# One more unit of the output projection ahead of the norms, in the first pair of the second feed-forward block

## The chip, the cores and the metric

The kernel runs on one core of one Trainium2 chip. The metric is the device time of one execution in microseconds. Five engines work side by side, each with an in-order queue: TensorE (PE, the matmuls, with their weight loads shown as PEld), VectorE (DVE), ScalarE (ACT), GpSimd (POOL) and SyncE (SP, which here only issues DMAs).

## What is computed

One inference step of one layer over 1024 prompt frames and 32 sample frames, 1056 rows of 1024 channels: a gated feed-forward block, a mixer (differential attention and a gated recurrence) and a second gated feed-forward block, each with a norm before and after it. The part around the change, cut from the reference:

```python
    out = jnp.concatenate([att_out, lru_out], axis=-1) @ w_out
    ...
    x = x + rmsnorm(m, gmb)                       # m is the mixer's out
    x = x + 0.5 * rmsnorm(swiglu(rmsnorm(x, g2a), f2g, f2u, f2d), g2b)
```

with `swiglu(x) = (silu(x @ w_gate) * (x @ w_up)) @ w_down`, an inner width of 2816, and everything in float32.

## The kernel before

Activations lie with channels on the 128 partitions and rows along the free dimension; the 1056 rows are split into two sides of 528 (`SB`) and four parts of 264 (`HB`). A float32 product is made of three matmuls on rounded parts (`mm3`, line 569: high times high, high times low, low times high), each 128x128 by 128x264.

`ffn` (line 852) is one feed-forward block. The inner width is walked in 11 pairs by `gate_up(p)`. Pair 0 of each block is the place where the block's input is made, and it is done in units, one for each of the four parts of the rows. A unit has three steps:

- **begin** (line 1557, second block): the part of the output projection that is still missing. For each of four column pairs c, 30 matmuls into a PSUM tile `po` (two halves, five of the eight inputs k = 7, 0, 1, 2, 3, three matmuls each), then VectorE adds the tile to `y` (line 1563) and `square_sum` squares it on ScalarE and sums it on VectorE into `acc`. A unit is 120 matmuls.
- **end** (line 1566): `boundary` (line 680) with the norm after the mixer. `rstd` (line 629) sums `acc` over partitions on TensorE, VectorE makes the mean (`ms`), GpSimd raises it to the power -1/2 (line 647), TensorE spreads the result over a PSUM tile `st`. Then for each c: load the residual tile `r` by DMA (line 685), scale `y` on VectorE, add `r`, store `y`, square and sum again. A second `rstd` gives the norm ahead of the block, and `scaled` applies it. After that `natural_operands` (line 713) splits the part into rounded high and low tiles `X`: casts on ScalarE, subtractions on VectorE.
- **products** (line 773): 48 matmuls for the gate and 48 for the up projection into PSUM tiles `pq`, with the weights `W`.

The loop at lines 873 to 885 places these: in turn n it writes the begin of unit n, then the end and the products of unit n - lead. With lead = 2 the order written is b0 b1 b2 e0 n0 b3 e1 n1 e2 n2 e3 n3 (b for begin, e for end, n for products). `sums` (line 891) then makes the seven combined operands that the later pairs use for a seven-product scheme (`right_operands`, line 718; `products`, line 805).

The order written is not the order run. A planner (lines 52 to 373) records every operation, finds what it depends on, and schedules all of them with a list scheduler whose priorities come from a backward pass; four rounds of six passes, the shortest modelled plan is kept, and each engine's queue is pinned to it. The order written enters in two ways: as the first priorities, and through the rings of buffers. `Ring` and `take` (lines 108 and 417) give a new tile only a slot whose last use stands earlier in the order written, and of these the one whose tile ends first by the plan of the round before. The tile then waits for that last use. Three rings matter here: `three`, three PSUM slots that `po` and `pq` share; `S`, 45 slots of SBUF that hold `cat` (the mixer's outputs, two slots for each k), `Wo` (the output projection's weights, two for each k), `y`, `X`, `W`, `H` and `r`; and `accp`, four slots for `acc`. While begin steps are still to come, ten slots of `cat` and ten of `Wo` are held.

```python
            lead = 2
            for n in range(len(units) + lead):
                if n < len(units):
                    s, (e, begin, _) = units[n]
                    begin(Z[s])
                if n >= lead:
                    s, (e, _, end) = units[n - lead]
                    ...
```

Of the kernel before, what the change touches and what calls it, by code (L numbers as in the profile page):

```python
# [498 lines left out]
def trunk(ctx: ExitStack, tc: tile.TileContext, plan, xt, w1g, w1u, w1d, w2g, w2u, w2d, win, wv, wout, kpast, vpast,  # L499
# [203 lines left out]
    def halves(t):  # L703

        v = t.rearrange("p a (e r) -> p a e r", e=2)
        return v[:, :, 0], v[:, :, 1]
# [6 lines left out]
    def natural_operands(Z, e, X):  # L713

        for h in range(2):
            X[h, e] = [operand(halves(Z[2 * h + c])[e], "X") for c in range(2)]
# [24 lines left out]
    def left_operands(src, natural=False):  # L741

        raw = []
        for s in src:
            raw.append(S.tile([128, 2, 512], F32, "raw"))
            sp.dma_start(raw[-1].rearrange("p a b -> p (a b)"), s)
        (a11, a12), (a21, a22) = ([r[:, 0], r[:, 1]] for r in raw)
        W = {}

        def make(i, a):  # L750
            t = S.tile([128, 2, 512], FR, "W")
            split((t[:, 0], t[:, 1]), a)
            W[i] = t[:, 0], t[:, 1]

        if natural:
            for k, a in (((0, 0), a11), ((1, 0), a21), ((0, 1), a12), ((1, 1), a22)):
                make(k, a)
            return W
        make(1, a11)
        make(4, a22)  # L760
        s3 = up.tile([128, 512], F32, "s3")
        adder.tensor_sub(s3, a11, a21)
        adder.tensor_add(a22, a21, a22)
        make(5, a22)
        make(2, a12)
        adder.tensor_sub(a11, a22, a11)
        make(6, a11)
        make(7, s3)
        adder.tensor_sub(a12, a12, a11)
        make(3, a12)  # L770
        return W

    def natural_products(ps, W, X, e, out, up_part):

        t = ps.tile([128, 2, 512], F32, "pq")
        for h in range(2):
            for r in range(2):
                for kk in range(4):
                    a, b = X[h, e][kk // 2], kk % 2
                    mm3(t[:, r, :HB], W[r, h], cslice(kk), (a[0][:, b], a[1][:, b]), slice(0, HB),  # L780
                        h == kk == 0, h == 1 and kk == 3)
        for r in range(2):
            if up_part:
                dve.tensor_mul(out[r], out[r], t[:, r, :HB])
            else:
                act.activation(out[r], t[:, r, :HB], AF.Silu)
# [65 lines left out]
    def ffn(tails, stat, sides, wg, wu, wd, cuts, finish, plain, last=False):  # L852
# [4 lines left out]
        def gate_up(p):  # L857
            H = [S.tile([128, 2, SB], F32, "H") for _ in range(2)]
            quarters = halves(H[0]) + halves(H[1])
            if p:  # L860
                for k, w in enumerate((wg, wu)):
                    W = left_operands([w[2 * p], w[2 * p + 1]], p < plain)
                    (natural_quarters if p < plain else products)(stat.four, W, X, quarters, k)
                    if k and p == plain - 1:
                        sums()
                return H, quarters
            W = [left_operands([w[0], w[1]], True) for w in (wg, wu)]
            place = stat.open(2)
            units = [(s, part) for s, tiles, parts in sides for part in parts]
            for s, tiles, _ in sides:  # L870
                Z[s] = tiles()

            lead = 2
            for n in range(len(units) + lead):
                if n < len(units):
                    s, (e, begin, _) = units[n]
# [3 lines that stand above are left out]
                    plan.hurry = HURRY[0]  # L880
                    end(Z[s])
                    natural_operands(Z[s], e, X[s])
                    plan.hurry = 0.0
                    for k in range(2):
                        natural_products(tails, W[k], X[s], e, [quarters[2 * r + e][:, s] for r in range(2)], k)
            place.close()
            if plain == 1:
                sums()
            return H, quarters

        def sums():
            for s, _, _ in sides:
                X[s] = right_operands(Z[s], X[s])
# [262 lines left out]
    def q_item(h):  # L1156
        def evac(p, tb):
            t = tp.tile([128, NT], F32, "tq")
            dve.scalar_tensor_tensor(t, p, -0.125 / SLOPES[h], rb[:, tsl(tb)], op0=ALU.mult, op1=ALU.mult)
            sp.dma_start(q_d[h][:, tsl(tb)], t)  # L1160
        return (h, evac)

    def k_item(h):
        def evac(p, tb):
            t = tp.tile([128, NT], F32, "tk")
            dve.tensor_mul(t, p, rb[:, tsl(tb)])
            sp.dma_start(k_d[h][:, tsl(tb)], t)
            sp.dma_start(k_o[h][:, tsl(tb)], t)
        return (4 + h, evac)
# [97 lines left out]
    def gate_item(c, h):  # L1267
        def evac(p, tb):
            g = tp.tile([128, NT], F32, "gl")
            dve.tensor_mul(g, p, rb[:, tsl(tb)])  # L1270
            act.activation(g, g, AF.Gelu_apprx_tanh)
            a = tb * NT
            n = min(NT, SEQ - a)
            adder.tensor_mul(g[:, :n], g[:, :n], h[:, a:a + n])
            if n < NT:
                adder.tensor_mul(g[:, n:], g[:, n:], h[:, S0:S0 + DEC])
            sp.dma_start(cat_d[4 + c][:, a:a + NT], g)

        return (16 + c, evac)
# [188 lines left out]
    def attend(h, head, stored, before, filler=(), per=0):  # L1468
        filler = iter(filler)
        if not stored:  # L1470
            cat[h] = pair(T, "cat%d" % h)
        for unit in ("s", 3, 2, 1, 0):
            plan.hurry = HURRY[2]
            if unit == "s":
                finish = attention_sample(h, head, cat[h])
            else:
                finish = attention_pair(h, unit, head, cat[h])
            if before is not None:
                before()
            plan.hurry = 0.0  # L1480
            before = finish
            for _ in range(per):
                next(filler, None)
        for _ in filler:
            pass
        return finish
# [11 lines left out]
    def out_group(ks, first):  # L1498
        for c in range(KD // 2):
            for s in range(2):  # L1500
                if first:
                    Y[c, s] = S.tile([128, 2, SB], F32, "y")
                for i in range(2):
                    for e in range(0, SB, HB):
                        p = one.tile([128, HB], F32, "po")
                        at = s * SB + e
                        for n, k in enumerate(ks):
                            mm3(p, Wo[k], cslice(2 * c + i), cat[k], slice(at, at + HB), n == 0, n == len(ks) - 1)
                        y = Y[c, s][:, i, e:e + HB]
                        if first:  # L1510
                            act.copy(y, p)
                        else:
                            dve.tensor_add(y, y, p)
                        yield

    def project_steps(items):
        for a in range(0, len(items), 2):
            yield from project(one, items[a:a + 2])

    def gates(*cs):  # L1520
        return project_steps([gate_item(c, H[c]) for c in cs])

    head = load_head(0)
    last = attend(0, head, True, None, project_steps([q_item(1), k_item(1), q_item(2), k_item(2)]), 3)
    head = load_head(1)
    last = attend(1, head, True, last, project_steps([q_item(3), k_item(3)] + [gate_item(0, H[0])]), 2)
    head = load_head(2)
    last = attend(2, head, False, last, gates(1, 2, 3), 2)
# [4 lines left out]
    last = attend(3, head, False, last, out_group((4, 5, 6), True), 7)  # L1533
# [133 lines left out]
```

## Time and profile before

| | |
|---|---|
| median of 3 runs | 1937.21 us (1936.35 to 1940.25) |
| the profiled execution | 1938.35 us |
| its span, first to last instruction | 1936.5 us |
| TensorE busy | 1901.5 us, 98% |
| VectorE busy | 1404.7 us, 73% |
| ScalarE busy | 685.3 us, 35% |
| GpSimd busy | 62.1 us, 3% |
| mean granted TensorE clock | 0.991 |

The profiled execution's own time is 1.85 us more than its span and 1.14 us above the median of the runs. The trace names every instruction by the tile it writes and the tiles it reads (`po<-cat7l,w` is a matmul of the output projection on the low part of input 7). All of them have line 145, the planner's call, so groups are told apart by tile. "Idle before" is what an engine waited just ahead of an instruction, with the one that released it. The granted clock (PEclk) is a share of full speed: 1.00 stands for 2.4 GHz and 0.50 for 1.2 GHz.

### The profile page before, as it was taken

How to read it: one execution, taken by the hardware profiler on the slowest of the kernel's cores; microseconds unless marked ns; L12 is line 12 of the kernel's file. 1: busy time of each engine (PE TensorE's matmuls, PEld its weight loads, DVE VectorE, ACT ScalarE, POOL GpSimd, SP SyncE). 2: the span in 40 equal slices, each digit the busy share in tenths (PEclk: the TensorE clock that was granted, in tenths of full speed). 3: DMA queues.
4: the chain of work that ended last, by engine and by line, in shares of the span. 5: the costliest groups of instructions: out<-in, count | busy, mean ns of one | idle time of the engine just before them, and what ended most of it. 6: DMA issues, size and time to landing. Idle time of an engine off the chain costs nothing.

```text
span 1936.5 us, 35396 instructions
## 1 busy us (share of the span) xinstructions
PE 1901.5 (98%) x14540; PEld 1861.9 (96%) x14540; DVE 1404.7 (73%) x2548; ACT 685.3 (35%) x1362; POOL 62.1 (3%) x79
## 2 busy tenths in 40 slices
PE   9999999999999999999999999999999999999997
PEld 8999999999999999988889899999999999999997
DVE  7866677665888587875767868886766666688847
ACT  7422222223233044453557655542222222333302
POOL 0000000000000001110000001100000000000000
PEclk9999999999999999999999999999999999999998
DMA  3332333324634243243452342323332223553442
GB/s 135 94 94 84 105 101 106 104 84 150 209 115 150 89 127 126 89 138 116 138 148 65 118 154 69 101 94 112 100 111 95 84 90 110 190 185 125 128 136 90
DMA packets 127810, 225.62 MB, mean 117 GB/s; under 512 B 11424, under 2 KB 84896, under 8 KB 127648
## 3 DMA queue, kind: packets, MB, share of 16 engines
q1 hardware_dynamic: 127504, 223.31, 36.3%
q8 instruction: 114, 1.87, 0.4%
q14 instruction: 48, 0.39, 0.1%
q10 hardware_dynamic: 144, 0.05, 0.0%
HBM read 157.48 MB, written 65.83 MB: 115 GB/s over the span
## 4 chain that ended last, share of the span: by engine, by line
PE 89%; DVE 5%; DMA 3%; ACT 1%; issue 1%; POOL 0%; SPq 0%; POOLq 0%; DVEq 0%; ACTq 0%
PE pq L145 43%; PE pd L145 19%; PE pp L145 8%; PE pe L145 5%; PE po L145 4%; PE pv L145 3%; PE st L145 3%; DVE y L145 1%; DVE W L145 1%; PE pg L145 1%; DMA raw<-q_d 1%; DVE X L145 0%; PE Sh0q L145 0%; PE Sh2q L145 0%; DMA t_d<-H 0%
## 5 line engine op out<-in xcount | busy, mean ns | idle before, releaser
L145 PE MATMUL pq<-X,W 128*128 128x264 f32 x7488 | 920.6, 285 | 2.4 <-DVE u L145 2.1
L145 PEld LDWEIGHTS pq<-X,W 128*128 128x128 f32 x7488 | 917.1, 189 | 3.4 <-DVE u L145 3.0
L145 PE MATMUL pd<-T,W 128*128 128x264 f32 x3024 | 368.7, 284 | 0.0
L145 PEld LDWEIGHTS pd<-T,W 128*128 128x128 f32 x3024 | 368.2, 188 | 0.0
L145 ACT CAST W<-raw 128x512 fp32r<-128x512 f32 x268 | 158.6, 603 | 421.5 <-PE pq L145 247.1
L145 DVE TENSOR_TENSOR W<-raw,W 128x512 fp32r<-128x512 f32 (+1 forms) x376 | 244.0, 672 | 2.7 <-ACT W L145 1.1
L145 DVE TENSOR_TENSOR u<-p,pq 128x528 f32<-128x528 f32 x80 | 56.3, 704 | 187.1 <-PE pq L145 187.1
L145 PE MATMUL pp<-xm,w 128*128 128x352 f32 x384 | 128.9, 336 | 5.9 <-DVE w L145 3.2
L145 PE MATMUL pp<-xm,wl 128*128 128x352 f32 x384 | 127.5, 333 | 0.7 <-DVE wl L145 0.7
L145 DVE TENSOR_TENSOR raw<-raw 128x512 f32<-128x512 f32 (+1 forms) x150 | 115.6, 773 | 14.8 <-DMA raw<-in_w1d 7.9
L145 ACT CAST T<-traw 128x528 fp32r<-128x528 f32 x80 | 48.7, 634 | 133.1 <-DMA traw<-t_d 100.1
L145 DVE TENSOR_TENSOR u<-u,pq 128x528 f32<-128x528 f32 x80 | 56.3, 704 | 46.9 <-PE pq L145 46.2
L145 DVE TENSOR_TENSOR T<-traw,T 128x528 fp32r<-128x528 f32 x126 | 84.4, 706 | 0.9
L145 PEld LDWEIGHTS pp<-xm,w 128*128 128x128 f32 x384 | 73.8, 192 | 8.9 <-issue 3.5
L145 PE MATMUL po<-cat,w 128*128 128x264 f32 x256 | 75.5, 298 | 2.4 <-DVE gl L145 1.0
L145 PEld LDWEIGHTS pp<-xm,wl 128*128 128x128 f32 x384 | 73.6, 192 | 1.8 <-DVE wl L145 1.4
L145 POOL TENSOR_TENSOR ms<-ms,neghalf 128x3 f32<-128x3 f32 x24 | 28.0, 1168 | 1472.3 <-DVE ms L145 1472.3
L145 PE MATMUL pe<-h,w 128*128 128x264 f32 x256 | 73.4, 287 | 0.0
L145 DVE TENSOR_TENSOR acc<-acc,sq 128x264 f32<-128x264 f32 x153 | 64.4, 432 | 11.9 <-ACT sq L145 10.4
L145 PE MATMUL po<-cat,wl 128*128 128x264 f32 x256 | 72.2, 287 | 0.6 <-DVE wl L145 0.6
L145 PE MATMUL pe<-h,wl 128*128 128x264 f32 x256 | 72.5, 286 | 0.0
L145 PE MATMUL pe<-hl,w 128*128 128x264 f32 x256 | 72.4, 284 | 0.0
(416 smaller groups left out, 2563.9 us busy)
## 6 DMA issues: line engine op xcount, KB each, us to landing
t_d<-H SPq DMA_DIRECT2D x126, 264.0 KB, 2.2
traw<-t_d SPq DMA_DIRECT2D x56, 528.0 KB, 4.6
raw<-in_w1g SPq DMA_DIRECT2D x22, 512.0 KB, 3.6
raw<-in_w1u SPq DMA_DIRECT2D x22, 512.0 KB, 3.9
raw<-in_w2g SPq DMA_DIRECT2D x22, 512.0 KB, 3.6
raw<-in_w2u SPq DMA_DIRECT2D x22, 512.0 KB, 3.7
raw<-in_w1d SPq DMA_DIRECT2D x36, 256.0 KB, 4.6
raw<-in_w2d SPq DMA_DIRECT2D x36, 256.0 KB, 4.6
```

Of the source, the lines that this page charges most:

```text
L145: self.made.append(f(*args, **kw).ins)
```

## The change

In the second block (`last` is true there) the loop of pair 0 runs with lead = 3; the first block keeps 2. The order written becomes b0 b1 b2 b3 e0 n0 e1 n1 e2 n2 e3 n3: the last unit of the output projection is written ahead of the first unit's norms and products, and nothing is added or removed.

```diff
@@ -870,7 +870,7 @@
             for s, tiles, _ in sides:
                 Z[s] = tiles()
 
-            lead = 2
+            lead = 3 if last else 2
             for n in range(len(units) + lead):
                 if n < len(units):
                     s, (e, begin, _) = units[n]
```

## Rows read from the trace of the kernel before

**Rows 1.** The page: busy us of each engine, and the granted clock by slices

```profile
PE 1901.5 (98%) x14540; PEld 1861.9 (96%) x14540; DVE 1404.7 (73%) x2548; ACT 685.3 (35%) x1362; POOL 62.1 (3%) x79
PEclk9999999999999999999999999999999999999998
```

**Rows 2.** Stretches of 50 us: busy PE, PEld, DVE, ACT, POOL; then PEclk

```profile
1200.00:1250.00 50.00, 46.77 (x359) 46.29 (x358) 40.73 (x87) 27.32 (x64) 6.58 (x4) 0.93 0.35 108
...
1300.00:1350.00 50.00, 50.00 (x413) 50.00 (x412) 35.37 (x57) 12.70 (x21) 0.00 (x0) 1.00 0.26 81
```

**Rows 3.** TensorE waits, 1195 to 1295: us in total, times, longest

```profile
PE st L145 <- POOL ms L145: 2.5, 1, 2.5
PE st L145 <- DVE acc L145: 1.0, 2, 0.7
PE pq L145 <- DVE u L145: 0.8, 1, 0.8
```

**Rows 4.** Short stretches, columns as rows 2; the sum covers 1198 to 1290

```profile
1198.00:1204.00 6.00, 6.00 (x52) 6.00 (x51) 5.60 (x13) 4.30 (x13) 0.00 (x0) 1.00 0.73 220
...
1204.00:1216.00 12.00, 12.00 (x101) 11.95 (x101) 10.22 (x24) 7.46 (x16) 1.95 (x2) 1.00 0.10 27
...
1234.00:1237.00 3.00, 0.50 (x4) 0.28 (x3) 2.05 (x4) 0.00 (x0) 2.76 (x1) 0.95 0.36 78
...
1237.00:1240.00 3.00, 3.00 (x15) 3.00 (x16) 0.58 (x2) 0.00 (x0) 0.85 (x1) 0.50 0.24 97
...
1240.00:1244.00 4.00, 4.00 (x22) 4.00 (x22) 1.54 (x4) 3.12 (x8) 0.00 (x0) 0.56 0.00 0
...
sum 92.00, PE 87.54 PEld 86.45 DVE 81.02 ACT 49.74 POOL 7.43; mean PE 6.73 PEld 6.65 DVE 6.23 ACT 3.83 POOL 0.57
```

**Rows 5.** TensorE by time: start, us, what, idle before (and releaser)

```profile
1198.09 6.37 PE L145 MATMUL pq<-X,W 128*128 128x264 f32 x51
...
1227.10 0.29 PE L145 MATMUL po<-cat,wl 128*128 128x264 f32 x1
...
1231.30 0.83 PE L145 MATMUL st<-ones,acc 128*128 128x1 f32 x6 [0.73 <-DVE acc L145]
...
1236.81 0.80 PE L145 MATMUL st<-ident,ms 128*128 128x128 f32 x2 [2.50 <-POOL ms L145]
...
1289.49 70.76 PE L145 MATMUL pq<-X,W 128*128 128x264 f32 x579 [0.80 <-DVE u L145]
```

**Rows 6.** The chain that ended last, 1216 to 1237: start, us, what

```profile
1216.42 6.23 PE po L145 x51
...
1222.67 0.36 SPq L145
...
1223.09 4.75 DMA r<-x_d
...
1232.97 3.80 POOL ms L145
```

**Rows 7.** Instructions on tile po: ns min/median/max, first and last start

```profile
L145 PEld LDWEIGHTS po<-cat7l,w x32: 187/188/192, 1139.0 to 1222.2; 128*128 128x128 f32 x32
```

**Rows 8.** GpSimd power steps: one by time, all 24 (min/median/max ns)

```profile
747.77 2.90 POOL L145 TENSOR_TENSOR ms<-ms,neghalf 128x3 f32<-128x3 f32 x1 [3.74 <-DVE ms L145]
...
L145 POOL TENSOR_TENSOR ms<-ms,neghalf x24: 841/878/3786, 15.4 to 1925.2; 128x3 f32<-128x3 f32 x24
```

**Rows 9.** VectorE in order of time, five pieces between 747 and 1265

```profile
747.59 2.37 DVE L145 TENSOR_TENSOR wl<-raw,w 128x1024 fp32r<-128x1024 f32 x2
...
1231.16 0.70 DVE L145 TENSOR_TENSOR y<-y,po 128x528 f32<-128x528 f32 x1
...
1234.11 1.94 DVE L145 TENSOR_TENSOR X<-y,X 128x528 fp32r<-128x528 f32 x3
...
1238.79 0.16 DVE L145 TENSOR_SCALAR ms<-st 128x3 f32<-128x3 f32 x1 [2.74 <-PE st L145]
...
1264.37 0.71 DVE L145 TENSOR_TENSOR X<-y,X 128x528 fp32r<-128x528 f32 x1
```

## The prediction, made before the changed kernel was run

> **What bounds the kernel now.** I read the page first: TensorE is busy 1901.5 us of 1936.5 [rows 1], so only work taken off TensorE, its idle time, or time at the lower clock can shorten the run. This change takes no work off, so I looked for the other two around the loop it edits. In stretches of 50 us, the one from 1200 has TensorE busy 46.8 us at a mean clock of 0.93, while 1300 to 1350 is full at 1.00 [rows 2]: the reader is to see that what can be won lies in that stretch, the middle of the edited loop. The waits name it: 2.5 us in one wait for GpSimd's power step, 1.0 us in two waits for sums on VectorE, 0.8 us for an add that empties a PSUM tile [rows 3]. In short stretches the idle time between 1198 and 1290 is 92 - 87.54 = 4.46 us, and behind the long wait the granted clock is 0.50 for three microseconds and 0.56 for four, with 0.95 in the three before [rows 4]: the lower level, 1.2 GHz. Of those 10 us, 3 x 0.50 + 4 x 0.44 + 3 x 0.05 = 3.4 us is lost. So the stretch loses 4.5 + 3.4 = 7.9 us. The order of time on TensorE shows that 0.73 + 2.50 us idle and the slow clock belong to one spot, 1230 to 1244 [rows 5]: 6.6 of the 7.9 us.
>
> **Why that spot is late.** TensorE ends the third unit's projection at 1198.1, takes up the first unit's products there, and does the last of the fourth unit's projection at 1227.1 [rows 5]; n0 (96 matmuls) thus lies among the matmuls of b3. The chain of waits shows what that costs: a matmul of `po` releases SyncE at 1222.67, it issues the load of an `r`, that lands 4.75 us later, and everything behind it, down to the power step at 1232.97 that TensorE stood for, hangs on the landing [rows 6]. The matmul that released it can be named: the last reader of the low part of input 7 starts at 1222.2 [rows 7]. By the source, 45 slots less 20 for `cat` and `Wo`, 8 for `y`, 8 for `W` and 2 for `H` leave 7 free while b3 runs, and e2's residual tiles stood in line for the slots that b3 holds. The last unit's chain is late by the same cause: b3's last add is at 1231.16, and e3's first mean at 1238.79 [rows 9].
>
> **The change, part by part.** It adds and removes no instruction, no DMA and no wait; it writes b3 before e0 and n0.
>
> TensorE: the work stays the same, 504 matmuls of the four units from 1198.1 on at 70.76 / 579 = 0.122 us [rows 5]. Only the order moves: n0, 96 x 0.122 = 11.7 us, goes behind b3. Price on TensorE zero, since b3's operands have all been ready for long and X of e0 merely waits. If that cover is gone, that is if `po` tiles aren't emptied in time, it costs what the last rival says.
>
> SyncE's queue: b3's matmuls end 11.7 us earlier, so the slot of input 7 is free at about 1222.4 - 11.7 = 1210.7, and the `r` that landed at 1223.09 + 4.75 = 1227.8 [rows 6] lands at 1215.5. The other loads of e2 and e3 move forward with it, past nothing but the stores of `y`, which are issued when `y` is done and not held by the loads. The loads then all meet between 1211 and 1216, eight at most, and I keep the 4.75 us for each.
>
> e2's second norm: its power step starts at 1232.97 [rows 6]; 11.7 us earlier would be 1221.3. VectorE will not allow all of it, as b3's adds come into the same time; taking half, 1227. b3 now ends at 1198.1 + 120 x 0.122 + 4 groups of statistic matmuls (estimated at 0.65 us each from the 0.83 us of one that overlaps the next matmul [rows 5]; so 2.6) = 1215.4, and behind it TensorE has n0 and n1, 23.4 us, to 1238.8, ready and asking nothing of e2; in the trace before it had n1 alone. The wait of 0.73 + 2.50 us and the clock behind it go: -6.6 us.
>
> e3: its first mean moves from 1238.79 by up to 11.7 us, to 1227.1. In the trace before, the last of its `X` is started at 1264.37 [rows 9], 25.6 us behind the mean; kept so, it would be ready at 1253.4. TensorE asks for it at 1198.1 + (120 + 288) x 0.122 + 8 x 0.65 = 1253.1, and needs only half of `X` for the first 48 matmuls, 5.9 us. It fits, with little to spare.
>
> What is late next: VectorE. It is busy 81.0 us of the 92 [rows 4], 11 us idle. 7 - 0.58 - 1.54 = 4.9 us of that idle time lies at 1237 to 1244 [rows 4] and is the echo of the stall, since VectorE waits there for the statistic that TensorE is late with; it goes with the stall. To follow a TensorE that is 5.6 us faster it must give up 0.7 us more, and it has 29% free in 1300 to 1350 [rows 2], so that some of its work can be left for later. So I charge nothing for it in the likeliest case; its bounds are 0 and, if it gives back only half of the echo, 2.8 us.
>
> GpSimd: the power steps are the one price that the trace shows only in scattered form. Of 24 the median is 0.88 us and the longest 3.79 [rows 8]. The long ones are explained by VectorE's row: three subtractions `X<-y,X`, both inputs in SBUF, run without a gap to 1234.11 + 1.94 = 1236.05 [rows 9], and the step ends at 1236.77 [rows 6], 0.7 us behind. In the first block the step of 2.90 us ends at 750.67 [rows 8], 0.7 us behind the end of two subtractions from SBUF at 749.96 [rows 9]. Three such steps move here (e2's second, both of e3's). The cost lies between 0 and 6.6 us, the loss seen here (2.5 + 0.73 + 3.4); the step of 2.90 us left the clock alone, so I take 1.0 us, nearer the lower end.
>
> The Trainium skill (SBUF — State Buffer, section "SBUF: two separate sides") states the rule behind those two rows: VectorE and GpSimd share one pair of ports, an instruction of VectorE with two SBUF inputs takes it for its whole length, and the other engine is blocked meanwhile. The trace agrees with 0.7 us twice. The rule speaks against this change, for a VectorE that is packed more tightly leaves GpSimd fewer gaps; taken strictly it would put the whole 6.6 us back, which is the first rival below.
>
> Sum: -6.6 + 1.0 = -5.6 us. Against the profiled execution that is 1938.35 - 5.6 = 1932.7; the median stands 1.14 us below that execution, so 1937.2 - 5.6 = **1931.6 us**. The other losses of the stretch (0.3 us in the second wait for sums, 0.8 for the add) are left as they are.
>
> **The rivals.** *The stall moves.* A power step of e2 or e3 falls again into a run of subtractions while the statistic matmul stands next in TensorE's queue. For it: the planner pins that matmul at the time it expects, and 2 of 24 steps were longer than 2 us. Against it: one of the two cost no clock. Time: 6.6 us come back, 1937.2 less some tenths, say 1937. Chance 0.20.
>
> *The order run doesn't follow the order written.* In the trace before, b3's matmuls already run on both sides of n0's; if the planner keeps products between the projection tiles, `r` gets its slot only a few microseconds sooner, and VectorE gives back half of its echo: 2.8 us, 1934.4. Against it: `po` and `pq` share three banks handed out in the order written, so n0's tile can come only behind b3's second to last tiles. Chance 0.12.
>
> *The banks fill, slower.* b3 no longer has products beside it, so its tiles come every 30 x 0.122 = 3.7 us on three banks, while VectorE is already busy 5.60 + 10.22 = 15.8 us between 1198 and 1216 [rows 4]. b3 brings four adds (0.62 us each) and seven sums (0.34), 4.9 us, so 20.7 us of work for the 17.2 us of b3 and its statistics. If VectorE serves them in the order they come, TensorE stands 3.5 us, and the clock falls for as long as it did in the trace: + 3.5 + 3.4 = 6.9 us, with the old stall left because e2 waits for the same engine: 1944. It decides from the point at which an add is more than two tiles, 7.3 us, late. Against it: e1's second scaling and e2's first can wait, since n1 is now 12 us further off. Chance 0.13.
>
> **How the numbers follow.** The forecast has 0.55, the rivals 0.20, 0.12 and 0.13. The planner computes every queue anew, so places elsewhere may shift by a microsecond or two in any of these cases. A measurement here can tell about 0.2%, 3.9 us, from no change. Faster by more than that: the forecast, with a little lost where a power step costs more than my 1.0 us: 0.55. Within: the first two rivals and the rest of the forecast, less a little that drifts out: 0.31. Slower: 0.14. The range goes from all 7.9 us won and a microsecond of drift, 1928.3, to the moved stall with the same drift upwards, 1938.5; it leaves out the slow rival and a tail below.
>
> **What would show it.** In the changed kernel's order of time on TensorE: all matmuls of `po` ended by about 1216, then four sets of products, with none of `po` between them; e2's last `r` landed by about 1218; e2's second power step by about 1227 and e3's first mean by the same time; the clock 1.00 in all short stretches from 1200 to 1260; VectorE idle at most 6 us between 1198 and 1284. The prediction is wrong if a power step of over 2 us stands ahead of a wait of TensorE again, if TensorE waits for `y` adds between 1198 and 1216, or if the first pairs behind 1255 begin with waits for VectorE.

## The result: slower, 1946.44 us for 1937.21

Over the runs of both kernels on one chip the changed kernel takes 1946.44 us in the median (1943.22 to 1951.90, 9 runs) and the kernel before 1937.21 (1934.09 to 1940.25, 9 runs): a ratio of 1.0056, 95% interval 1.0046 to 1.0066. The forecast was 1931.6 with a range up to 1938.5. The sign was wrong and the time lies outside the range.

The profiled execution of the changed kernel took 1951.9 us (span 1950.1). That is 5.5 us above its median, while that of before is 1.1 above; so the shares below hold for these two executions, 13.6 us of span apart, and the medians are 9.2 apart. The stages are cut at the first matmul on the low part of input 7 (`po<-cat7l`, the start of b0) and at the last products of pairs 0 and 1, found by counting matmuls.

| stage | before, us | after, us | difference |
|---|---|---|---|
| start to b0 | 1139.2 | 1142.5 | +3.3 |
| b0 to the end of pair 0 (the edited loop) | 134.5 | 138.4 | +3.9 |
| pair 1 | 42.4 | 44.7 | +2.3 |
| pair 2 to the end | 620.5 | 624.5 | +4.0 |

The loop was to become 5.6 us shorter and became 3.9 longer. The rest is spread over stages that the edit doesn't touch in the source; the planner redraws every queue, and even the order in the first block differs. TensorE's idle time ahead of b0 is 20.8 us for 16.7, and behind pair 1 it is 15.3 for 13.3.

The page of after, its busy times and the granted clock by slices, against [rows 1]:

```profile
PE 1904.0 (98%) x14540; PEld 1863.4 (96%) x14540; DVE 1418.7 (73%) x2584; ACT 663.1 (34%) x1324; POOL 67.2 (3%) x79
...
PEclk9999999999999999999999899999999999999998
```

TensorE has the same matmuls and 2.5 us more busy time. VectorE has 36 instructions and 14.0 us more, ScalarE 38 and 22.2 us fewer, since the planner also chooses anew which of the two does some copies and casts; in the loop their work is the same as before. One slice more stands below 0.9. The stretches of 50 us of after (busy PE, PEld, DVE, ACT, POOL; then PEclk), with the whole edited loop in the last line:

```profile
1200.00:1250.00 50.00, 45.62 (x360) 44.81 (x359) 36.74 (x77) 24.08 (x57) 7.19 (x4) 0.97 0.24 77
1250.00:1300.00 50.00, 46.24 (x356) 45.74 (x356) 44.35 (x81) 23.01 (x47) 3.10 (x1) 0.94 0.32 98
...
1142.00:1281.00 139.00, 131.09 (x1044) 129.52 (x1044) 110.38 (x224) 69.75 (x166) 15.36 (x10) 0.98 0.29 92
```

and the same loop of before:

```profile
1139.00:1274.00 135.00, 130.96 (x1045) 129.52 (x1045) 111.02 (x225) 69.85 (x165) 13.24 (x10) 0.97 0.31 97
```

Busy time is equal, 131.09 and 130.96 us, so the 4 us of the loop are idle time of TensorE: 7.9 us for 4.0 (the lower clock costs some 3.4 us in both). The stretch from 1200, which stood at 46.77 us [rows 2], now has 45.62, and the next one is as bad. Where TensorE stands, in its order of time (start, us, what, idle before and releaser):

```profile
1198.68 0.36 PE L145 MATMUL po<-cat,w 128*128 128x264 f32 x1 [1.53 <-DVE y L145]
...
1218.52 0.29 PE L145 MATMUL po<-cat,wl 128*128 128x264 f32 x1
1218.64 1.13 PE L145 MATMUL pq<-X,W 128*128 128x264 f32 x8
...
1225.47 1.22 PE L145 MATMUL st<-ident,ms 128*128 128x128 f32 x6 [1.93 <-POOL ms L145]
...
1243.21 0.80 PE L145 MATMUL st<-ones,acc 128*128 128x1 f32 x6 [1.86 <-DVE acc L145]
...
1262.20 0.83 PE L145 MATMUL st<-ident,ms 128*128 128x128 f32 x6 [1.67 <-POOL ms L145]
...
1297.53 2.76 PE L145 MATMUL pq<-X,W 128*128 128x264 f32 x11 [2.09 <-ACT W L145]
```

The order asked for is there: the projection ends at 1218.52 and the first products start behind it. But in place of one spot with 0.73 + 2.50 us [rows 5] there are four of 1.5 to 1.9, for a PSUM add, a power step, a sum and a power step again. Behind the second and the fourth the clock is at its lower level (short stretches of after, columns as above):

```profile
1226.00:1229.00 3.00, 3.00 (x16) 3.00 (x15) 2.28 (x5) 1.52 (x3) 0.00 (x0) 0.50 0.84 278
1263.00:1267.00 4.00, 4.00 (x22) 4.00 (x22) 3.76 (x6) 3.58 (x8) 0.00 (x0) 0.57 0.00 0
```

**What came late.** The waits of SyncE's queue in after, 1185 to 1225 (us in total, times, longest):

```profile
SPq L145 <- PE po L145: 21.5, 4, 18.0
```

the same of before, 1185 to 1230:

```profile
SPq L145 <- PE po L145: 4.0, 2, 2.9
```

and the issues of that queue in after, in order of time:

```profile
1180.63 0.46 SPq L145 DMA_DIRECT2D r<-x_d  x1
1194.44 1.60 SPq L145 DMA_DIRECT2D x_d<-y  x3
1214.10 4.91 SPq L145 DMA_DIRECT2D r<-x_d  x5
```

SyncE stands 18.0 us for one matmul of the projection before it issues five loads of `r`. The first of the five is not one of e2's but the fourth of e1's, as VectorE's order shows (after):

```profile
1193.71 1.94 DVE L145 TENSOR_TENSOR y<-y,r 128x528 f32<-128x528 f32 x3
...
1216.41 0.70 DVE L145 TENSOR_TENSOR y<-y,po 128x528 f32<-128x528 f32 x1 [4.04 <-PE po L145]
1217.03 0.70 DVE L145 TENSOR_TENSOR y<-y,r 128x528 f32<-128x528 f32 x1
...
1244.56 0.15 DVE L145 TENSOR_SCALAR ms<-st 128x3 f32<-128x3 f32 x1
```

Three of e1's residual adds run at 1193.7; the fourth at 1217.0, ahead of e2's four. The planner's own list of slots says why (its times are a model's, here some 24 us ahead of the chip's):

| e1's fourth `r` | slot held before by | last use of that starts | loaded | its last use starts | last use of e1's third `r` starts |
|---|---|---|---|---|---|
| before | e1's own first `r` | 1174.9 | 1175.6 | 1179.5 | 1176.9 |
| after | `Wo` of input 7, read until the end of b3 | 1189.9 | 1190.2 | 1193.3 | 1171.7 |

In the plan, too, the fourth is 21.6 us behind the third. The slot was taken by the book of the round before, which had this use of `Wo` end ahead of the last use of e1's own first `r`; by the time the queues were drawn it was the other way round. GpSimd's power steps show what follows from it (after):

```profile
1222.18 3.24 POOL L145 TENSOR_TENSOR ms<-ms,neghalf 128x3 f32<-128x3 f32 x1 [14.49 <-DVE ms L145]
1232.78 1.24 POOL L145 TENSOR_TENSOR ms<-ms,neghalf 128x3 f32<-128x3 f32 x1 [7.37 <-DVE ms L145]
1244.79 1.86 POOL L145 TENSOR_TENSOR ms<-ms,neghalf 128x3 f32<-128x3 f32 x1 [10.77 <-DVE ms L145]
1259.04 3.10 POOL L145 TENSOR_TENSOR ms<-ms,neghalf 128x3 f32<-128x3 f32 x1 [12.38 <-DVE ms L145]
```

e1's second step comes at 1222.18 (1206.19 before), e2's second at 1232.78 (1232.97 before) and e3's first at 1244.79 (1239.03 before); three norms now queue on VectorE one behind the other.

### The profile page after: what moved, and what is told of

It is laid out like the page before. It is cut to its first block, busy times and chain, and to the rows that moved or that the text cites. A ratio compares the mean times of both kernels' runs of the same rounds, so it can differ in the third digit from the quotient of the medians.

```text
span 1950.1 us, 35362 instructions
## 1 busy us (share of the span) xinstructions
PE 1904.0 (98%) x14540; PEld 1863.4 (96%) x14540; DVE 1418.7 (73%) x2584; ACT 663.1 (34%) x1324; POOL 67.2 (3%) x79
## 4 chain that ended last, share of the span: by engine, by line
PE 86%; DVE 6%; DMA 3%; issue 2%; ACT 2%; POOL 1%; POOLq 0%; DVEq 0%; SPq 0%; ACTq 0%
PE pq L145 42%; PE pd L145 19%; PE pp L145 8%; PE pe L145 5%; PE po L145 3%; PE st L145 2%; PE pv L145 2%; DVE y L145 1%; DVE W L145 1%; DMA t_d<-H 1%; DMA raw<-in_w2u 1%; POOL ms L145 1%; DVE H L145 1%; DMA x_d<-y 1%; DVE acc L145 1%
## 5 line engine op out<-in xcount | busy, mean ns | idle before, releaser
L145 ACT CAST W<-raw 128x512 fp32r<-128x512 f32 (+1 forms) x263 | 157.8, 608 | 418.1 <-PE pq L145 260.8
L145 DVE TENSOR_TENSOR raw<-raw 128x512 f32<-128x512 f32 (+1 forms) x150 | 115.4, 773 | 13.6 <-DMA raw<-in_w1d 6.8
```

Source lines behind the costliest of these rows:

```text
L145: self.made.append(f(*args, **kw).ins)
```

## The experiments

The theories that the expectations weigh: the **slot** of e1's fourth residual makes the loss (S); the **order** itself makes it, whatever the slots (O); the planner's reshuffle of everything else makes it (P); the **banks**, a run of projection tiles that VectorE doesn't empty (B), with the rival that a gain there is given back since VectorE is full (D); the **hold** of the power step, which the planner's book has at 0.8 us (H). The last three kernels ask whether the cures do without the lead (C), need it (L), or whether it is luck of the plan. Each ratio is to runs of before taken in the same round, whose medians are 1937.1 to 1937.4 us. A kernel with a rule for slots has three lines more ahead of the planner's call, so its line is 148. Medians and ratios:

| kernel | lead | what else | median, us | ratio, 95% |
|---|---|---|---|---|
| after | 3 | | 1946.44 | 1.0046 to 1.0066 |
| slot3 | 3 | slot rule | 1941.71 | 1.0011 to 1.0029 |
| pass3 | 3 | 7 passes | 1942.24 | 1.0019 to 1.0038 |
| pass2 | 2 | 7 passes | 1937.31 | 0.9996 to 1.0014 |
| slot2c | 2 | bad slot forced | 1955.98 | 1.0084 to 1.0111 |
| add3 | 3 | slot rule, adds first | 1942.23 | 1.0017 to 1.0036 |
| add2 | 2 | adds first | 1942.56 | 1.0016 to 1.0042 |
| cost3 | 3 | slot rule, adds first, longer power step in the book | 1932.37 | 0.9967 to 0.9988 |
| cost2 | 2 | longer power step in the book | 1952.65 | 1.0063 to 1.0093 |
| all2 | 2 | adds first, longer power step | 1936.81 | 0.9989 to 1.0008 |
| cost3n | 3 | longer power step | 1934.82 | 0.9984 to 1.0001 |
| cost3p | 3 | as cost3, 7 passes | 1938.99 | 1.0001 to 1.0018 |

### slot3: lead 3, and e1's residuals may not take slots of the projection's inputs

```diff
-    def take(self, name, ring):
+    def take(self, name, ring, rule=None):
+        if rule is not None:
+            found = [f for f in found if rule(ring.holds[f[1]] or "")] or found
...
+            plan.rule = (lambda h: not h.startswith(("cat", "w_", "wl_"))) if res is x1_d and a == SB else None
...
-            lead = 2
+            lead = 3 if last else 2
```

> lead 3, and one rule more for the planner: the four residual tiles of the second unit's norm (e1) are never given a slot of cat or Wo, which b3 holds. Theory S (the slot): in the changed kernel e1's fourth residual stood 18 us for a slot of b3, and everything behind e1 was late by that; here SyncE's 18 us wait is gone, e1's second power step lies near 1207 and not at 1222, the stretch from the first matmul on input 7 to the end of the pair's products is 4 to 8 us shorter than in the changed kernel, and the median is 1936 to 1941. Theory P (the planner's reshuffle of everything else): the median stays 1943 to 1948. Theory O (the order itself, b3 without products beside it): e1 is early, but the stretch stays as long as in the changed kernel, 1943 to 1948.

Measured: 1941.71 us, 4.7 less than after and still 0.20% above before. e1's second power step is at 1196.78 (after: 1222.18) and e2's second at 1226.77, so the norms run as early as the prediction had them. But the loop is no shorter: 141.7 us from b0 to the end of pair 0, where 4 to 8 us less than in after were expected. Nor is SyncE's long wait for the projection gone (slot3, 1185 to 1235):

```profile
SPq L148 <- PE po L148: 24.9, 3, 24.3
```

It now stands ahead of the loads of e2 and e3 alone, issued from 1216.87 on. So such a wait is no fault in itself; which load stands behind it counts. Now the banks fill. TensorE's order of time in slot3:

```profile
1194.43 0.56 PE L148 MATMUL po<-cat,w 128*128 128x264 f32 x1 [3.40 <-DVE y L148]
```

VectorE in slot3, the adds that empty `po`:

```profile
1175.75 0.70 DVE L148 TENSOR_TENSOR y<-y,po 128x528 f32<-128x528 f32 x1
...
1193.59 0.69 DVE L148 TENSOR_TENSOR y<-y,po 128x528 f32<-128x528 f32 x1
...
1194.55 0.69 DVE L148 TENSOR_TENSOR y<-y,po 128x528 f32<-128x528 f32 x1
```

For 17.8 us VectorE works at e1's norm and empties no tile; then it does three adds in a row. The clock around it (slot3, columns as before):

```profile
1192.00:1194.00 2.00, 0.00 (x0) 0.00 (x0) 2.00 (x5) 2.00 (x6) 0.00 (x0) 0.83 0.36 127
1194.00:1200.00 6.00, 5.57 (x26) 5.60 (x27) 5.26 (x13) 3.05 (x9) 0.98 (x1) 0.50 0.02 6
1200.00:1202.00 2.00, 2.00 (x17) 2.00 (x17) 2.00 (x4) 1.46 (x3) 0.00 (x0) 0.96 0.00 0
```

The bank wait thus costs 3.40 us idle and about 2.8 more at 0.50 (5.57 x 0.5). And the old stall stands where it stood, though e2's second power step now starts 6.2 us earlier than before. GpSimd and TensorE in slot3:

```profile
1226.77 3.58 POOL L148 TENSOR_TENSOR ms<-ms,neghalf 128x3 f32<-128x3 f32 x1 [18.01 <-DVE ms L148]
1230.40 1.04 PE L148 MATMUL st<-ident,ms 128*128 128x128 f32 x6 [2.27 <-POOL ms L148]
```

From 1231.0 to 1237.6 the clock is at 0.50 again. An early e2 is not enough to end that wait: the step itself is long, 3.58 us.

The median lies between what S and O expected. With the slot rule half of the 9.2 us is gone, but not in the loop: in the profiled executions slot3 gains on after ahead of b0 (9 us) and behind pair 0, where its plan differs as well. That the slot itself is worth 4.7 us is therefore not shown.

### pass3 and pass2: seven passes of the planner, with lead 3 and with lead 2

```diff
-    ROUNDS, PASSES = 4, 6
+    ROUNDS, PASSES = 4, 7
```

> lead 3 with nothing changed but the planner's passes in a round, 7 for 6, so that it ends in another plan; in that plan e1's fourth residual reuses the slot of e1's first. Theory S: like the kernel with the rule, 1936 to 1941, with no long wait of SyncE before 1210. Theory P: anywhere within 8 us of 1946, and not tied to the residual. Theory O: 1943 to 1948.

> lead 2 with 7 passes for 6: what a new plan alone does to the time. Theory S: within 3 us of the kernel before, 1934 to 1940, since here too e1's fourth residual reuses e1's first slot. Theory P: off by 5 us or more, either way.

Measured: pass3 1942.24, pass2 1937.31. With seven passes the plan of lead 3 gives e1's fourth residual the slot of its first by itself, without the rule, and the median falls by 4.2 us, nearly as with slot3: the same slot reached in two ways. The loop is again no shorter than in after (138.8 us), and SyncE again waits long for the projection (22.0 us), which S had excluded. The hole in front of the banks is there too. The adds of pass3 leave a hole from 1176.8 to 1195.5, and TensorE stands behind it for a sum (pass3, order of time):

```profile
1195.68 1.41 PE L145 MATMUL st<-ones,acc 128*128 128x1 f32 x6 [3.16 <-DVE acc L145]
```

pass2 says that one more pass by itself is worth nothing at lead 2. The fault of the slot is not in the order written: with lead 2 as with lead 3, e1's norm is written behind b3 and might take a slot of `Wo`. It is the draw of one plan.

### slot2c: the bad slot put into the old order

```diff
+            plan.rule = (lambda h: h.startswith("cat0_")) if res is x1_d and a == SB and c == 3 else None
```

> lead 2, and e1's fourth residual tile is made to take a slot of cat[0], whose last reader is a late matmul of b3: the suspected cause alone, in the old order. Theory S: SyncE stands 15 us or more for a projection matmul, e1's second power step moves from 1206 to 1225 or later, the pair ends 4 us or more later, and the median is 1941 to 1950. Theories P and O: 1937 within 4 us, as the order written is the old one.

Measured: 1955.98 us, 18.8 above before, more than expected. SyncE's issues in slot2c:

```profile
1224.69 1.91 SPq L148 DMA_DIRECT2D r<-x_d  x4
```

VectorE's order of time:

```profile
1202.16 1.95 DVE L148 TENSOR_TENSOR y<-y,r 128x528 f32<-128x528 f32 x3
...
1230.78 0.71 DVE L148 TENSOR_TENSOR y<-y,r 128x528 f32<-128x528 f32 x1 [0.78 <-DMA r<-x_d]
```

and TensorE's:

```profile
1233.88 1.44 PE L148 MATMUL st<-ones,acc 128*128 128x1 f32 x6 [5.44 <-DVE acc L148]
```

The slot is that of `cat` of input 0, last read at 1224.9. By the planner's order e1's fourth residual is the second of the four loads from 1224.69 on and its add the one at 1230.78, 27 us behind the third. TensorE then stands 5.44 us for a sum, and from 1233.7 to 1250.6 the clock is at 0.50, which alone is 8.5 us. The loop takes 147.9 us, 13.4 more than before, and pair 1 5.8 more. Such a slot, with the plan that is drawn around it, costs more here than the whole change did. A reason may be that with lead 2 b3 ends later (last `po` at 1228.2, after: 1218.5) and so holds e1 longer. The long wait of SyncE for a projection matmul that I expected isn't there, since the loads of e2 stood ahead of this one in its queue, the first of them 10.1 us for products, and took up the time.

### add3 and add2: the adds that empty `po` come first

```diff
+                    plan.hurry = HURRY[0]
                     dve.tensor_add(yp(c), yp(c), p[:, :, :HB])
+                    plan.hurry = 0.0
```

add3 has this beside slot3's edits, add2 alone with lead 2.

> lead 3, the rule that keeps e1's residual tiles off b3's slots, and the adds of the projection tiles to y (which empty the three banks) given first place among ready work on VectorE. Theory B (the banks): with the slot cured, lead 3 still loses 3.4 us of idle time at 1194 and some 3 us of half clock behind it, since VectorE did e1's norm for 18 us before it emptied a bank; here that wait is under 1 us, the clock between the first projection matmul and the first product is 1.00, the idle time of that stretch falls from 4.7 us to under 2.5, and the median from 1941.7 to 1935 to 1938.5. Rival D (VectorE is the bound): what the adds gain e1 loses, the idle time reappears behind 1225, and the median stays 1940 to 1943.

> lead 2 with the same first place for the adds: the control. Theory B: the old order has n0's products between b2 and b3 and lost only 0.5 us before the first product, so 1935 to 1939.5, no more than 2 us from the kernel before. Rival D: the same, or up to 4 us slower.

Measured: add3 1942.23, add2 1942.56. In add3 no wait for an add is left, the clock is 1.00 and the loop shrinks from 141.7 to 134.9 us. Not all of that is the banks': no power step of over 1.6 us is left in this plan either, and TensorE's wait for one is at most 0.3 us. The median is that of slot3. Pair 1 gives the gain back (add3: the stretches from b0 to the first products, the rest of pair 0, and pair 1; columns as before):

```profile
1137.00:1219.00 82.00, 80.12 (x646) 78.40 (x645) 66.42 (x137) 39.49 (x99) 7.90 (x7) 1.00 0.32 99
1219.00:1272.00 53.00, 51.17 (x420) 50.66 (x419) 43.53 (x88) 31.41 (x68) 3.27 (x3) 1.00 0.29 93
1272.00:1319.00 47.00, 43.35 (x338) 42.69 (x337) 37.72 (x63) 13.81 (x23) 0.00 (x0) 0.96 0.39 120
```

TensorE in add3, at the start of pair 1:

```profile
1275.64 0.63 PE L148 MATMUL pq<-X,W 128*128 128x264 f32 x3 [3.21 <-DVE W L148]
```

VectorE is late with the next pair's weights: 3.21 us idle, and pair 1 takes 47.0 us for 42.4. That is the median of rival D, though it is not e1 that pays: the bank wait can be removed, and the gain is not kept. (The loop gained 6.8 us in the profiled execution and pair 1 lost 5.0; b0 began 3.6 later.) That the adds themselves make the weights late is not shown: in add2 and cost3, which have them first too, pair 1 takes 41.6 and 41.9 us. With lead 2 the same edit costs 0.29%, more than either expectation had.

### cost3 and cost2: the planner's book gets a power step of 2.8 us

```diff
-        return 300 + 165 * n
+        return 2300 + 165 * n
```

cost3 has this beside add3's edits, cost2 alone with lead 2.

> add3, and the planner is told that GpSimd's power step takes 2.0 us longer than it was told so far, so that it pins the statistic matmul behind it later in TensorE's queue and puts products ahead of it. Theory H (the held power step): TensorE's waits for that step in the pair fall from 2.3 to 3.5 us to under 1 us, with the half clock behind them, 3 to 6 us: 1930 to 1935. Rival D: the second norms of e2 and e3 are themselves late, TensorE stands for X instead, and the median is that of add3 within 1.5 us.

> lead 2 with the same longer power step in the planner's book. Theory H: the wait of 2.5 us at 1236 and the half clock behind it, 6 us, shrink to under 2: 1931 to 1935. Rival D: in the old order the chain of e2 is late by itself and TensorE has only n1 beside it, so the wait returns as a wait for X: 1935 to 1941.

Measured: cost3 **1932.37 us**, 0.12 to 0.33% faster than before; cost2 1952.65, 0.78% slower. In cost3 the steps are not shorter, they are in other places. GpSimd in cost3:

```profile
1202.14 3.79 POOL L148 TENSOR_TENSOR ms<-ms,neghalf 128x3 f32<-128x3 f32 x1 [15.97 <-DVE ms L148]
1215.33 5.44 POOL L148 TENSOR_TENSOR ms<-ms,neghalf 128x3 f32<-128x3 f32 x1 [9.40 <-DVE ms L148]
```

TensorE in cost3:

```profile
1214.48 4.38 PE L148 MATMUL pq<-X,W 128*128 128x264 f32 x34
1220.82 0.83 PE L148 MATMUL st<-ident,ms 128*128 128x128 f32 x6 [1.95 <-POOL ms L148]
```

Stretches of cost3, ten microseconds around that wait and all of pair 0 behind the projection:

```profile
1215.00:1225.00 10.00, 8.05 (x66) 7.84 (x66) 8.37 (x20) 4.57 (x10) 5.44 (x1) 1.00 0.46 155
1213.00:1269.00 56.00, 53.10 (x436) 52.46 (x435) 52.53 (x108) 32.59 (x71) 8.53 (x4) 1.00 0.31 102
```

With 34 products placed between the sum and the spread, a step of 5.44 us costs TensorE 1.95 us and no clock, and that of 3.79 us 0.33. The loop takes 130.6 us, 3.9 less than before: in this plan most of the forecast's 5.6 us is there. Nearly all of it is the clock, for the idle time of the loop is 3.8 us (before: 4.0), and the waits for power steps are 2.3 us in all, where under 1 was expected.

What the wait follows can be read from all the kernels. With the short step in the book, 13 power steps of the loop last over 1.5 us, in before, pass2, add2, after, slot3, pass3 and add3, at lead 2 and 3, with e2 early and late. TensorE waits for every one of them, 1.2 to 1.4 us less than the step lasts: so much work it still had when the step began, in a plan that takes a step to last 0.8 us. With 2.0 us more in the book it waits 3.5 us less than the step lasts in cost3 and cost3p, and in cost2, all2 and cost3n it waits for no step, though all2 has one of 3.81 us and cost2 one of 2.83. So the wait goes by the length of the step and by what stands beside it, and not by how late e2 is.

But cost2 shows that the same longer number makes the plan of lead 2 much worse, which neither expectation had: 6.4 us of waits for sums and no wait for a power step, of 9.9 us idle in the loop. Its waits (cost2, 1142 to 1332):

```profile
PE st L145 <- DVE acc L145: 6.4, 3, 2.9
```

Why that plan has its sums so late was not settled.

### all2, cost3n and cost3p: is it the lead?

all2 has add2's and cost2's edits together with lead 2. cost3n has lead 3 and the longer power step alone. cost3p is cost3 with seven passes.

> lead 2 with first place for the adds and the longer power step in the planner's book (the slot rule has nothing to do in the old order). Theory L (lead 3 is worth some 5 us once its costs are cured): 1938 or more, as in the old order TensorE has only n1 beside e2's chain. Theory C (the cures alone made the fast kernel): 1930 to 1935.

> lead 3 with the longer power step in the planner's book alone, without first place for the adds and without the slot rule (in this plan e1's fourth residual reuses e1's first slot anyway). Theory B (the banks cost by themselves): 2 us or more of idle time ahead of the first product, and 1936 to 1942. Rival: the booking was all that was wanted, 1930 to 1934.5.

> the fast kernel (lead 3, slot rule, first place for the adds, longer power step) with 7 passes for 6 in the planner: does its gain survive another plan. Theory L: 1930 to 1936. If it was one lucky plan: 1937 or more.

Measured: all2 1936.81, cost3n 1934.82, cost3p 1938.99. all2 and cost3n lie between their two expectations, and cost3p is where one lucky plan was to show. The cures without the lead give nothing against before, in the one plan tried, so they are not by themselves what makes cost3 fast. cost3n reaches 0.08% less than before (no clear difference) with 5.1 us idle from b0 to the first product, 3.4 of it for sums and 1.1 for an add that empties a bank; in its plan e1's fourth residual has the slot of its first. And cost3p is cost3 with another draw: its loop is as short, 130.5 us, so the gain in the loop holds in both plans, but b0 starts 3.0 us later, pair 1 takes 42.9 us for 41.9, and the median is 6.6 us higher. So the lead, cured of the slot, gives between -0.22% and +0.29% in six plans (slot3, pass3, add3, cost3, cost3n, cost3p). That lead 3 is faster in itself is not shown; nor that it is slower. Among the kernels with lead 3 only the one with the bad slot, the changed kernel itself, is clearly slower than that spread.

The loop alone says more than the medians (one profiled execution of each kernel). With nothing beside it lead 3 takes 138.4 and 138.8 us (after, pass3) where lead 2 takes 134.5 and 135.2 (before, pass2). With adds first it takes 134.9 for 139.7 (add3, add2), with the longer step in the book 135.4 for 142.3 (cost3n, cost2), and with both 130.6 and 130.5 for 135.9 (cost3, cost3p, all2). So in these plans the lead lengthens its own loop by some 4 us when it comes alone, and shortens it by 5 to 7 beside a cure for the waits that the forecast put at nothing or at 1.0 us.

## Why the prediction was wrong, point by point

**What bounds the kernel: right. Why TensorE stood there: wrong, and this is the step that failed.** The chain from the late `r` to the power step at 1232.97 was read rightly. But TensorE stood for the end of that step, which lasted 3.79 us. With the median of 0.88 us [rows 8] it would have ended at 1233.85, before TensorE ran out of work at 1236.81 - 2.50 = 1234.31 [rows 5]. "The wait of 0.73 + 2.50 us and the clock behind it go", the -6.6 us of the sum, was drawn from an earlier e2 alone. In slot3 e2's second step starts at 1226.77, as worked out, and 2.27 us of wait with the lower clock behind it stand there all the same.

**Power steps charged 1.0 us: too low.** In after the loop waits 1.93, 1.67 and 0.53 us for them with two spells at half clock: 3.0 x 0.50 + 4.0 x 0.43 = 3.2 us, together 7.3, somewhat more than the 6.6 that had gone. So the first rival (0.20), the stall that moves, happened, and it is the largest part of the miss. Idle time and half clock of the loop were to fall from 7.4 to 1.8 us and came to 11.3. Of the 9.5 us between, the power steps make 6.3; nearly all the rest is the wait of 1.86 us for a sum and that of 1.53 for a PSUM add. The rival's reason held: the steps of 3.24 and 3.10 us stand in VectorE's work from SBUF; the first of them ends at 1225.42, 0.7 us behind a run without a gap that ends at 1224.70.

**SyncE's queue: wrong too.** The prediction counted 7 free slots and moved "the other loads of e2 and e3" past nothing but stores. It looked at the loads that wait and not at the choice that makes a load wait. That choice is drawn anew in every plan, and here it gave e1's fourth residual, not waiting in the trace before, a slot that b3 holds. e2's loads did move as worked out: issued from 1214.10, predicted 1210.7 from a b0 that starts 3.3 us later. (The landing at 1215.5 left out the 0.7 us from the matmul to the start of the load; nothing hangs on it.) But they came behind e1's, into a VectorE that had e1's norm to do first. With another slot the medians are 4.7 and 4.2 us lower (slot3, pass3), but their loops are no shorter than that of after, so the size of this term stays open. slot2c shows that a bad slot can be dear, +18.8 us with the plan around it.

**e2's and e3's norms: late.** e2's second power step was to start at about 1227 and started at 1232.78; e3's first mean at 1227.1, and came at 1244.56, although b3's last add starts at 1220.37 (before: 1231.16 [rows 9]). In slot3 e2's second step is at 1226.77, as worked out.

**TensorE's price zero for b3 in one piece: wrong.** "If `po` tiles aren't emptied in time" was named as the cover and it did go: 1.53 us idle in after, 3.40 in slot3, and 3.16 for a sum behind the same hole in pass3. The rival that was given 0.13 had its price right: 3.5 us idle and 3.4 of clock, where slot3 measured 3.40 and about 2.8. What was wrong is the reason against it, that e1's second scaling can wait: the planner let the adds wait and did e1's norm. That rival also kept the old stall, as slot3 does. slot3's loop is 7.2 us longer than before, where the rival had 6.9; the median stands at 1941.7, the rival at 1944.

**VectorE charged at zero: wrong.** In after TensorE waits 1.53 us for an add and 1.86 for a sum, both VectorE's, and in pair 1 2.09 us for ScalarE's cast of weights, which itself had waited 3.80 us for VectorE. add3 has 3.21 us of wait for weights there. So the free 29% of 1300 to 1350 [rows 2] was no reserve in these plans: pair 1's weights fall due ahead of it.

**The order run: right.** The projection ended at 1218.5 (predicted 1215.4, plus the 3.3 us of the later start), with four sets of products behind it and no `po` between them.

**The signs and the range.** Of the three signs of being wrong the first two came as written, a power step of over 2 us ahead of a wait and a wait for `y` adds at 1198.68, and the third in part (pair 1's wait for weights). The range was cut as though the cases exclude each other. Two rivals and an unnamed fault came together, and VectorE has a part in each. And a new plan moves the time by more than "a microsecond or two": cost3 and cost3p, one pass apart, are 6.6 us apart.

What stays open: how much of the +3.3 us ahead of b0 and the +4.0 behind pair 1 in the profiled execution is more than such a draw, what the slot of e1's fourth residual is worth by itself, and why cost2 is so slow. Of the 9.2 us of the median only the 3.9 us of the loop are explained wait by wait.

## What to carry to other kernels

Where a planner hands out shared buffers from a plan of the round before, a change of order has two effects, the one meant and a new draw; before the gain is judged, compare who holds the slot of each late load in the two plans, and draw the plan more than once. Read the length that the planner gives its own plan, too: 1898.5 us before and 1902.0 after, so its model already had the new order 3.5 us behind. Before a stall is put down to what is late, compare its length with the step that it waits for: here the planner's book had the step too short, and the wait stayed wherever the step moved. A unit moved forward takes away the products that had given VectorE time to empty its banks: price the longest hole between two emptying adds, and where the next stage's weights stand in the same queue. A long wait in the queue of SyncE for a matmul does not tell a bad slot by itself (18.0 us in after, 24.3 in slot3, where e1's loads are early): look at which load is issued behind it, and who needs that one first.

## What the hardware showed that was not expected

A power step of three elements per partition takes 0.85 us alone and 5.44 us in cost3, where VectorE works without a gap at adds and subtractions from SBUF from 1215.17 to 1220.07; it ends at 1220.77, 0.7 us behind, as in the two cases of the prediction. This agrees again with the Trainium skill (SBUF — State Buffer, section "SBUF: two separate sides"); the trace adds that GpSimd was held here over ten instructions of VectorE in a row, not over one. The step of 3.79 us at 1202.14 in cost3 ends at 1205.93, again 0.7 us behind the last VectorE instruction with both inputs in SBUF (1205.22), though VectorE goes straight on with an add that reads PSUM.

Idle times of nearly one length are not followed by one clock. It stayed at 1.00 behind 1.95 us in cost3 and behind 1.53 and 1.86 us in after. It was 0.50 for some 3 us behind 1.93 and 1.67 us in after and, from two microseconds after TensorE had taken up work again, behind 2.50 in pass2 and 3.21 in add3. It was 0.50 for over 6 us behind 2.50 in before, 2.27 in slot3 and 3.40 in slot3. A sum that adds the clock behind each stall has to leave both ends open.
